# Joining two of the three matmuls of each weight block into one of 512 columns, in the four residual projections of a two-block layer

## The chip, the cores and the metric

The kernel runs on one core of one Trainium2 chip. Its metric is the device time of one execution in microseconds (us), the median of a few runs. Five engines work side by side, each through its own instructions in their written order: TensorE (PE, whose weight loads are listed apart as PEld), VectorE (DVE), ScalarE (ACT), GpSimd (POOL) and SyncE (SP), which here only issues DMA transfers. They wait for each other through semaphores.

## The reference

Two transformer blocks for 256 tokens of width 1024, in float32. What matters here are the four projections whose result is added to the residual stream, and the norm that follows each:

```
# block 1
h = h + merged @ w_out                       # 1024 x 1024   ("wo")
u = rmsnorm(h);  z = silu(u @ w_gate) * (u @ w_up)
h = h + z @ w_ffn_down                       # 2816 x 1024   ("wd")
x = rmsnorm(h)
# block 2
h = rmsnorm(x) * (1 + sc_m) + sh_m
x = x + g_m * (concat(y_ssd, y_att) @ w_out2)   # 1024 x 1024 ("wo2")
h = rmsnorm(x) * (1 + sc_f) + sh_f
x = x + g_f * (conv_ffn(h) )                 # its last product, 2816 x 1024, is "wd2"
return rmsnorm(x)
```

## The kernel before

**Layout and tiling.** Activations are kept with features on the 128 partitions and the 256 tokens (S) along the free dimension, in tiles [128, 8, 256]: eight groups of 128 features. A product is made one output group at a time: `gemm` walks over 128x128 weight blocks and accumulates in one PSUM bank. So wo and wo2 have 8 output groups of 8 blocks, wd and wd2 8 output groups of 22 blocks: 480 blocks in the four projections.

**Split precision.** Each factor is held as a high and a low part in the format fp32r. `wload` fetches 128x1024 weights by DMA (`raw`), ACT rounds them to `wh`, DVE forms the rest `wl` (both tiles have 5 buffers). An activation has a tile for its high part and one for its low part (`xg2h` and `xg2l`, `uf1h` and `uf1l`, and so on). `mm3` makes three matmuls of 256 columns for a block: `wh` by high, `wh` by low, `wl` by high, all into the same 256 columns of the bank. The bank has room for 512.

**Around a residual projection.** When the bank of group f is complete, DVE adds it to the residual (`tt` into `h`, or `stt` into `x1` with the gate as a factor). ACT and DVE then make the high and low part of the scaled group (`scaled`, into `xg2`, `xg3`, `xg4`), and its squares are summed (`Stats`, tile `acc`). The first four products after the norm are made from these scaled but not yet normed groups (96 matmuls, `gemm_multi`, with features 6 and 7 last). In the middle of them PE multiplies `acc` by a matrix of ones, and ACT makes the factor r = exp(-0.5 ln(mean square)) in two instructions. With r, `normed` makes the normed activation group by group: DVE `un`, ACT the high part, DVE the low part (`uf1`, `u2`, `uf2`). The next products read those.

**Order.** The program is recorded, then put in an order by a list scheduler with fixed weights (`OPT`), and each engine gets its instructions in that order. A change of one operation can so move others.

Of the kernel before, what the change touches and what calls it, by code (L numbers as in the profile page):

```python
# [16 lines left out]
P = 128  # L17
S = 256
# [31 lines left out]

# The program is first recorded (operations on symbolic tiles), then put in an order by a list
# scheduler, and then emitted in that order.

# weights of the list scheduler (microseconds; la and altw in nanoseconds)
OPT = dict(
# [13 lines left out]

# products of the first blocks after a norm: the last features come last  # L70
PARTS = [list(range(6)), [6, 7]]
# [70 lines left out]
class Program:  # L142
# [7 lines left out]

    # tiles
    def tile(self, shape, dtype, tag, name, bufs=1, pool="sb"):
# [6 lines left out]

    # operations  # L160
    def op(self, eng, dur, fn, reads, writes, table=None, key=None, nbytes=0):
# [57 lines left out]
    def either(self, out, in_, scale=None, bias=None, func=AF.Copy, key=None):  # L219
        # out = scale * in + bias on ScalarE or on VectorE  # L220
        o = self.act(out, in_, func, bias=bias, scale=scale, key=key)
        nap = sum(isinstance(x, Ref) for x in (bias, scale))
        dur = out.n * (1.0417 if in_.t.psum else 0.5208) + 68 + 61 * nap

        def f():
            v = self.nc.vector
            if scale is None and bias is None:
                v.tensor_copy(out.real(), in_.real())
            elif bias is None:
                v.tensor_scalar(out=out.real(), in0=in_.real(), scalar1=_real(scale), scalar2=None, op0=ALU.mult)  # L230
            elif scale is None:
                v.tensor_scalar(out=out.real(), in0=in_.real(), scalar1=_real(bias), scalar2=None, op0=ALU.add)
            else:
                v.tensor_scalar(out=out.real(), in0=in_.real(), scalar1=_real(scale), scalar2=_real(bias), op0=ALU.mult, op1=ALU.add)

        o.alts["DVE"] = (dur, f, None)
        return o
# [69 lines left out]

    # order
    def schedule(self):
# [31 lines left out]
        def gate(o):  # L341
            # earliest time at which the tiles of o can be had; None when a tag is used up
            g = 0.0
            need = None
            for t in o.tiles:
                if not t.live:
                    k = (t.pool, t.tag)
                    if t.bufs == 1 and t.seq != nxt[k]:
                        return None
                    need = need or defaultdict(int)  # L350
                    need[k] += 1
            if need:
                for k, n in need.items():
                    sf = slot_free[k]
                    if len(sf) < n:
                        return None
                    g = max(g, sorted(sf)[n - 1])
            return g
# [109 lines left out]
def record(pr, d):  # L468
# [13 lines left out]
    def bank2():  # L482
        return bank([P, 2, S])

    def pair(tag, name):
        return big(tag + "h", name + "h", F32R), big(tag + "l", name + "l", F32R)

    def pair_sh(tag, name, m0):
        x = big(tag + "h", name + "h", F32R, [P, KD, S + 2]), big(tag + "l", name + "l", F32R, [P, KD, S + 2])
        sh = mod[:, m0:m0 + 8].rearrange("p (k o) -> p k o", o=1).to_broadcast([P, KD, 2])  # L490
        act(x[0][:, :, S:S + 2], sh, AF.Copy)
        tt(x[1][:, :, S:S + 2], sh, x[0][:, :, S:S + 2].bitcast(F32), ALU.subtract)
        return x

    def hl_of(t):
        return lambda k: (t[0][:, k, :], t[1][:, k, :])

    def memset(t, val):
        pr.op("POOL", 300, lambda: nc.gpsimd.memset(t.real(), val), [], [t], key=-1.0)

    # parameters and constants
    cst_t = pr.tile([P, NCST], F32, "cst", "cst_t")
    vec_t = pr.tile([P, NV], F32, "vec", "vec_t")
    row_t = pr.tile([P, NR0], F32, "row", "row_t")
    bv_t = big("ml", "bv_t", shape=[P, 1152])
    crow = pr.tile([P, D], F32, "crow", "crow")
# [36 lines left out]

    # building blocks
    def wload(src, n):
# [9 lines left out]
    def mm3(ps, w, i, hl, k, first, last):  # L555
        hi, lo = hl(k)
        a, b = w[0][:, i * P:(i + 1) * P], w[1][:, i * P:(i + 1) * P]
        pr.group([(ps, a, hi, first, False), (ps, a, lo, False, False), (ps, b, hi, False, last)])

# [109 lines left out]

    # attention of two heads  # L670
    def attn_pair(q, krows, vcols, bias, init, sink, yh, yl):
# [44 lines left out]

# [1 line left out]
    h = big("h", "h")  # L718
# [19 lines left out]
    def v_third(t3):  # L738
        pv = [bank() for _ in range(2)]
        for c in range(4):  # L740
# [9 lines left out]
            for k2 in range(2):  # L750
                k = 2 * c + k2
                a, b = wh[:, k2 * 384:(k2 + 1) * 384], wl[:, k2 * 384:(k2 + 1) * 384]
                for i in range(2):
                    hi, lo = xg[0][:, k, i * P:(i + 1) * P], xg[1][:, k, i * P:(i + 1) * P]
                    o = pv[i][:, :384]
                    pr.group([(o, hi, a, k == 0, False), (o, hi, b, False, False), (o, lo, a, False, k == 7)])
# [22 lines left out]

    # gates and queries of the recurrence  # L780
    A_all = big("yhh", "A_all", shape=[P, 4, 2, S])
    K_all = big("yhl", "K_all", shape=[P, 4, 2, S])
    Q_all = big("ml", "Q_all", shape=[P, 4, 2, S])
    on = big("mh", "on")
    wi = d["wi"]
# [35 lines left out]
    def hgrn_pair(p):  # L821
# [27 lines left out]
        tt(Q, B, Q, ALU.mult)  # L849
        # scores in blocks of two chunks: within the chunks, then from the second chunk to the first  # L850
        aT = aTs[p % 2]
# [25 lines left out]
        either(ST, ps[:, 0:2])  # L877
        # outputs by token, so that the norm of a head is a scalar of the partition
        o = bank([P, 2, 2, P])
# [58 lines left out]

    # output gate of the recurrence
    hgs = []  # L940
# [8 lines left out]

    # merge of the branches  # L950
    dma(crow, d["rows"][0:1, NR - 1024:NR].to_broadcast([P, D]), D * 512, key=pr.T - 40)
# [33 lines left out]
    for f in range(KD):  # L985
        b = bank2()
        gemm(b[:, 0, :], d["wo"][f], hM)
        tt(h[:, f, :], b[:, 0, :], h[:, f, :], ALU.add)
        scaled(xg, h, gffn, f)
        st2.add(h[:, f, :])  # L990

    def ztiles(name, tags):
        zh = [big(t + "h", f"{name}h{i}", F32R) for i, t in enumerate(tags)]
        zl = [big(t + "l", f"{name}l{i}", F32R) for i, t in enumerate(tags)]
        return zh, zl

# [13 lines left out]
    hl = hl_of(u)  # L1010
    zh, zl = ztiles("z", ("m", "ya", "yh"))
    for p in range(NFF // 2):
# [17 lines left out]
        t, o = divmod(2 * p, 8)  # L1030
        split(zh[t][:, o:o + 2, :], zl[t][:, o:o + 2, :], sg)
    tt(g1e, V("norm_final_g", 0, 8), V("norm_final_g", 0, 8), ALU.mult)
# [6 lines left out]
    st3 = Stats(KD, lambda f: g1e[:, f:f + 1], tail=False)  # L1039
    hz = lambda k, zh=zh, zl=zl: (zh[k // 8][:, k % 8, :], zl[k // 8][:, k % 8, :])  # L1040
    for f in range(KD):
        b = bank2()
        gemm(b[:, 0, :], d["wd"][f], hz, NFF)
        tt(h[:, f, :], b[:, 0, :], h[:, f, :], ALU.add)
        scaled(xg, h, fmix, f)
# [7 lines left out]

# [1 line left out]
    w2 = d["w2"]  # L1055
    xbc = big("yhl", "xbc")
    NG = 4
# [49 lines left out]

    tz = big("yhh", "tz")
    dma(tz, d["toep"], 2048 * 512)
# [5 lines left out]
    for hf in range(2):  # L1115
        pv = [bank() for _ in range(2)]
        for c in range(2):
            wh, wl = wload(d["w2v"][hf, c], 1040)
            for k4 in range(4):
                k = 4 * c + k4  # L1120
                a, b = wh[:, k4 * 260:(k4 + 1) * 260], wl[:, k4 * 260:(k4 + 1) * 260]
                for i in range(2):
                    hi, lo = u[0][:, k, i * P:(i + 1) * P], u[1][:, k, i * P:(i + 1) * P]
                    o = pv[i][:, :260]
# [9 lines left out]
    def ssd():  # L1134
# [48 lines left out]
        either(prev, ps)  # L1183
        m_all = big("mh", "m_all", shape=[P, 2, 2, 4, P])
        ce_all = big("ml", "ce_all", shape=[P, 2, 4, P])
        for i in range(2):
# [69 lines left out]
    ob = [bank2() for _ in range(NG)]  # L1256
    gemm_multi(ws3, [b[:, 0, :] for b in ob], hY, [[4, 5, 6], [7], [0, 1, 2, 3]])
    st4 = Stats(KD, tail=False)
    ffac, sffn = (lambda f: fac[:, 1, f:f + 1]), (lambda f: mod[:, 24 + f:25 + f])
    xg = pair_sh("ya", "xg4", 24)  # L1260
    for f in range(8):
        if f < NG:
            b = ob[f]
        else:
            b = bank2()
            gemm(b[:, 0, :], d["wo2"][f], hY)
        stt(x1[:, f, :], b[:, 0, :], mod[:, 16 + f:17 + f], x1[:, f, :], ALU.mult, ALU.add)
        scaled(xg, x1, ffac, f)
# [7 lines left out]
    with Chain("n4"):  # L1276
        normed(u, x1, ffac, r, sffn)
    zh, zl = ztiles("z2", ("m", "yh", "ya"))
    for f in range(NFF):
# [14 lines left out]
        tt(t[:, 0, :], t[:, 0, :], t[:, 1, :], ALU.mult)  # L1294
        split(zh[f // 8][:, f % 8, :], zl[f // 8][:, f % 8, :], t[:, 0, :])
    st5 = Stats(KD)
    act(rc0, t[:, 0, 0:1], AF.Ln, bias=eps[:, 0:1], scale=0.0)
    hz2 = lambda k: (zh[k // 8][:, k % 8, :], zl[k // 8][:, k % 8, :])
    ot = big("uh", "ot")
    for f in range(8):  # L1300
        b = bank2()
        gemm(b[:, 0, :], d["wd2"][f], hz2, NFF)
        stt(x1[:, f, :], b[:, 0, :], mod[:, 40 + f:41 + f], x1[:, f, :], ALU.mult, ALU.add)
        st5.add(x1[:, f, :])
# [111 lines left out]
```

## Time and profile before

| | |
|---|---|
| median of 3 runs | 804.1 us (803.27 to 804.19) |
| span of the profiled execution | 801.7 us |
| its own time | not given apart; the median stands 2.4 us above the span |
| PE busy | 791.0 us, 99% |
| DVE busy | 604.7 us, 75% |
| ACT busy | 497.3 us, 62% |
| mean granted TensorE clock | 0.997 |

The span runs from the first to the last instruction of the profiled execution. Busy times count overlapped stretches of one engine once. Matmuls overlap each other, so that the duration of one (0.28 us) says little and the distance between two starts says what one costs.

### The profile page before, as it was taken

How to read it: one execution, taken by the hardware profiler on the slowest of the kernel's cores; microseconds unless marked ns; L12 is line 12 of the kernel's file. 1: busy time of each engine (PE TensorE's matmuls, PEld its weight loads, DVE VectorE, ACT ScalarE, POOL GpSimd, SP SyncE). 2: the span in 40 equal slices, each digit the busy share in tenths (PEclk: the TensorE clock that was granted, in tenths of full speed). 3: DMA queues.
4: the chain of work that ended last, by engine and by line, in shares of the span. 5: the costliest groups of instructions: out<-in, count | busy, mean ns of one | idle time of the engine just before them, and what ended most of it. 6: DMA issues, size and time to landing. Idle time of an engine off the chain costs nothing.

```text
span 801.7 us, 16002 instructions
## 1 busy us (share of the span) xinstructions
PE 791.0 (99%) x6362; PEld 759.5 (95%) x6362; DVE 604.7 (75%) x1104; ACT 497.3 (62%) x910; POOL 2.2 (0%) x13
## 2 busy tenths in 40 slices
PE   8999999999999999999999999999999999999996
PEld 7998999899999999999999999977799999999995
DVE  6985876778767788776768869966378988987552
ACT  6688999884445675444444559566466866556451
POOL 1000000000000000000000000000000000000000
PEclk9999999999999999999999999999999999999998
DMA  8945424459787658988778984652334666665731
GB/s 276 334 146 158 126 86 132 131 181 339 259 281 255 183 160 289 328 277 282 261 250 286 327 273 135 190 179 82 97 109 138 202 200 209 200 181 148 214 94 53
DMA packets 47803, 161.39 MB, mean 201 GB/s; under 512 B 5600, under 2 KB 8304, under 8 KB 47600
## 3 DMA queue, kind: packets, MB, share of 16 engines
q1 hardware_dynamic: 47728, 160.37, 62.6%
q8 instruction: 50, 0.82, 0.4%
q14 instruction: 25, 0.20, 0.1%
HBM read 159.03 MB, written 1.06 MB: 200 GB/s over the span
## 4 chain that ended last, share of the span: by engine, by line
PE 97%; DMA 1%; SPq 1%; DVE 0%; ACT 0%; issue 0%; DVEq 0%
PE ps L292 87%; PE ps L284 8%; PE ps L299 2%; DMA raw<-in_wv_dram 1%; SPq L305 1%; DVE ot L255 0%; DVE wl L255 0%; ACT r L215 0%; ACT wh L215 0%; DVE x L261 0%; ACT sql L215 0%; DVEq L1411 0%
## 5 line engine op out<-in xcount | busy, mean ns | idle before, releaser
L215 ACT ACTIVATE wh<-raw 128x1024 fp32r<-128x1024 f32 (+3 forms) x253 | 256.9, 1021 | 211.1 <-PE ps L292 144.1
L255 DVE TENSOR_TENSOR wl<-raw,wh 128x1024 fp32r<-128x1024 f32 (+3 forms) x257 | 300.3, 1175 | 81.8 <-ACT wh L215 78.1
L292 PE MATMUL ps<-u1h,wh 128*128 128x256 f32 x360 | 106.8, 297 | 0.0
L292 PE MATMUL ps<-u1h,wl 128*128 128x256 f32 x360 | 101.3, 281 | 0.0
L292 PE MATMUL ps<-u1l,wh 128*128 128x256 f32 x360 | 101.0, 280 | 0.0
L292 PE MATMUL ps<-uf2h,wl 128*128 128x256 f32 x320 | 90.1, 282 | 0.0
L292 PE MATMUL ps<-uf1h,wl 128*128 128x256 f32 x320 | 90.1, 282 | 0.0
L292 PE MATMUL ps<-uf2h,wh 128*128 128x256 f32 x320 | 89.8, 281 | 0.0
L292 PE MATMUL ps<-uf1h,wh 128*128 128x256 f32 x320 | 89.8, 280 | 0.0
L292 PE MATMUL ps<-uf1l,wh 128*128 128x256 f32 x320 | 89.7, 280 | 0.0
L292 PE MATMUL ps<-uf2l,wh 128*128 128x256 f32 x320 | 89.7, 280 | 0.0
L261 DVE SCALAR_TENSOR_TENSOR raw<-raw,crow 128x1024 f32<-128x1024 f32 x48 | 58.5, 1222 | 40.5 <-DMA raw<-in_wada_dram 40.4
L292 PEld LDWEIGHTS ps<-u1h,wh 128*128 128x128 f32 x360 | 68.0, 189 | 2.2 <-issue 1.5
L292 PEld LDWEIGHTS ps<-u1l,wh 128*128 128x128 f32 x360 | 67.9, 189 | 0.0
L292 PEld LDWEIGHTS ps<-u1h,wl 128*128 128x128 f32 x360 | 67.7, 188 | 0.0
L292 PEld LDWEIGHTS ps<-uf1h,wh 128*128 128x128 f32 x320 | 60.6, 189 | 0.0
L292 PEld LDWEIGHTS ps<-uf2h,wh 128*128 128x128 f32 x320 | 60.5, 189 | 0.0
L292 PEld LDWEIGHTS ps<-uf2l,wh 128*128 128x128 f32 x320 | 60.2, 188 | 0.0
L292 PEld LDWEIGHTS ps<-uf1l,wh 128*128 128x128 f32 x320 | 60.2, 188 | 0.0
L292 PEld LDWEIGHTS ps<-uf2h,wl 128*128 128x128 f32 x320 | 60.1, 188 | 0.0
L292 PEld LDWEIGHTS ps<-uf1h,wl 128*128 128x128 f32 x320 | 60.1, 188 | 0.0
L292 PE MATMUL ps<-zh,wh 128*128 128x256 f32 x176 | 49.5, 281 | 0.0
(320 smaller groups left out, 2048.0 us busy)
## 6 DMA issues: line engine op xcount, KB each, us to landing
raw<-in_wi_dram SPq DMA_DIRECT2D x49, 512.0 KB, 4.6
raw<-in_wada_dram SPq DMA_DIRECT2D x48, 512.0 KB, 4.6
raw<-in_wup_dram SPq DMA_DIRECT2D x44, 512.0 KB, 4.3
raw<-in_wd_dram SPq DMA_DIRECT2D x32, 512.0 KB, 4.3
raw<-in_wg_dram SPq DMA_DIRECT2D x22, 512.0 KB, 4.5
raw<-in_wu_dram SPq DMA_DIRECT2D x22, 512.0 KB, 5.0
raw<-in_w_dram SPq DMA_DIRECT2D x20, 512.0 KB, 4.4
raw<-in_wo_dram SPq DMA_DIRECT2D x16, 512.0 KB, 3.7
```

The source lines that it names most:

```text
L215: self.nc.scalar.activation(out.real(), in_.real(), func, **kw)
L255: f = lambda: self.nc.vector.tensor_tensor(out=out.real(), in0=in0.real(), in1=in1.real(), op=op)
L261: self.nc.vector.scalar_tensor_tensor(out=out.real(), in0=in0.real(), scalar=_real(scalar), in1=in1.real(), op0=op0, op1=op1, **kw)
L284: f = lambda: self.nc.tensor.matmul(out.real(), lhsT.real(), rhs.real(), start=start, stop=stop)
L292: self.nc.tensor.matmul(out.real(), a.real(), b.real(), start=start, stop=stop)
L299: f = lambda: self.nc.tensor.transpose(out.real(), in_.real(), ident.real())
L305: f = lambda: self.nc.sync.dma_start(out=_real(out), in_=_real(src))
```

## The change

High and low part of an activation become the two halves of one tile [128, 8, 2, 256]. Where the PSUM tile given to `mm3` has 512 columns, one matmul multiplies `wh` by both parts, the high part's products going to the bank's first half and the low part's to its second, and the matmul of `wl` by the high part goes to the second half. The bank is then added to the residual in two instructions, one for each half. This is done in wo, wd, wo2 and wd2; all other products keep three matmuls of 256 columns. Tiles that shared buffers with the two parts (`A_all` and `K_all`, `xbc` and `tz`, and others) are joined in pairs in the same way. `OPT` is the same.

```diff
-        hi, lo = hl(k)
+        hi, lo, both = hl(k)
         a, b = w[0][:, i * P:(i + 1) * P], w[1][:, i * P:(i + 1) * P]
-        pr.group([(ps, a, hi, first, False), (ps, a, lo, False, False), (ps, b, hi, False, last)])
+        if ps.n == 2 * S:
+            calls = [(ps, a, both, first, last), (ps[:, 1, :], b, hi, False, False)]
+            pr.group(calls[::-1] if last else calls)
+        else:
+            pr.group([(ps, a, hi, first, False), (ps, a, lo, False, False), (ps, b, hi, False, last)])
...
-        gemm(b[:, 0, :], d["wo"][f], hM)
-        tt(h[:, f, :], b[:, 0, :], h[:, f, :], ALU.add)
+        gemm(b, d["wo"][f], hM)
+        for e in range(2):
+            tt(h[:, f, :], b[:, e, :], h[:, f, :], ALU.add)
...
-        gemm(b[:, 0, :], d["wd2"][f], hz2, NFF)
-        stt(x1[:, f, :], b[:, 0, :], mod[:, 40 + f:41 + f], x1[:, f, :], ALU.mult, ALU.add)
+        gemm(b, d["wd2"][f], hz2, NFF)
+        for e in range(2):
+            stt(x1[:, f, :], b[:, e, :], mod[:, 40 + f:41 + f], x1[:, f, :], ALU.mult, ALU.add)
```

The order of the instructions moves at the two places where wo and wo2 hand over to the feed-forward products.

DVE behind wo, before: from the last sum of squares on, r is used in `un`, and `uf1l` is the low part of the normed activation.

```order
L261 SCALAR_TENSOR_TENSOR un<-h,vec_t,r 128x256 x3
L255 TENSOR_TENSOR uf1l<-un,uf1h 128x256 x3
L261 SCALAR_TENSOR_TENSOR un<-h,vec_t,r 128x256 x3
L255 TENSOR_TENSOR uf1l<-un,uf1h 128x256 x2
L261 SCALAR_TENSOR_TENSOR un<-h,vec_t,r 128x256 x2
L255 TENSOR_TENSOR uf1l<-un,uf1h 128x256 x3
L255 TENSOR_TENSOR wl<-raw,wh 128x1024 x3
```

The same place now (`uf_3686` is the joined tile of both parts):

```order
L261 SCALAR_TENSOR_TENSOR un<-h,vec_t,r 128x256 x3
L255 TENSOR_TENSOR sg<-ps,r 128x256
L255 TENSOR_TENSOR wl<-raw,wh 128x1024
L255 TENSOR_TENSOR uf_3686<-un,uf_3686 128x256 x3
L261 SCALAR_TENSOR_TENSOR un<-h,vec_t,r 128x256 x3
L255 TENSOR_TENSOR wl<-raw,wh 128x1024
L255 TENSOR_TENSOR uf_3686<-un,uf_3686 128x256 x3
L261 SCALAR_TENSOR_TENSOR un<-h,vec_t,r 128x256 x2
L255 TENSOR_TENSOR wl<-raw,wh 128x1024
L255 TENSOR_TENSOR uf_3686<-un,uf_3686 128x256 x2
```

Three weight roundings and one product with r, which stood behind the whole normed activation, now stand between its parts.

ACT behind wo2, before: the two steps of r, then the high parts of the normed activation (`uf2h`).

```order
L215 ACTIVATE r<-ps,eps 128x256
L215 ACTIVATE r<-r 128x256
L215 ACTIVATE uf2h<-un,mod 128x256 x6
L215 ACTIVATE wh<-raw 128x1024 x2
L215 ACTIVATE uf2h<-un,mod 128x256 x2
```

And now:

```order
L215 ACTIVATE wh<-raw 128x1024
L215 ACTIVATE r<-ps,eps 128x256
L215 ACTIVATE wh<-raw 128x1024
L215 ACTIVATE r<-r 128x256
L215 ACTIVATE wh<-raw 128x1024 x2
L215 ACTIVATE uf_7286<-un,mod 128x256 x8
```

Four weight roundings, two of them behind the first high parts before, now stand ahead of all of them. On DVE in the same place two roundings stand ahead of the first `un`, one behind it.

PE behind wo2, now: from the product of the squares with ones (`acc_7001`) to the first matmuls of the normed activation.

```order
L284 MATMUL ps<-acc_7001,ones_d 128x256
L292 MATMUL ps<-xg_6876,wh 128x258 x2
L292 MATMUL ps<-xg_6876,wl 128x258
L292 MATMUL ps<-xg_6876,wh 128x258 x2
L292 MATMUL ps<-xg_6876,wl 128x258
L292 MATMUL ps<-xg_6876,wh 128x258 x2
L292 MATMUL ps<-xg_6876,wl 128x258
L292 MATMUL ps<-xg_6876,wh 128x258 x2
L292 MATMUL ps<-xg_6876,wl 128x258
L292 MATMUL ps<-uf_7286,wh 128x256 x2
```

Of the 96 matmuls with the unnormed `xg`, 84 now stand ahead of the product with ones and 12 behind it; before, 39 stood ahead and 57 behind. Behind wo it is 66 and 30 now, and was 36 and 60. Behind wd it is 36 and 60 in both. In both kernels the block order behind the 12 (or 30) is: three blocks of the first normed product, some of the second, and only then the first product's groups 3 to 7, with 14 blocks in all up to group 7.

## Rows read from the trace of the kernel before

**Rows 1.** The page: span, and the first engines' busy time, share and instructions.

```profile
span 801.7 us, 16002 instructions
...
PE 791.0 (99%) x6362; PEld 759.5 (95%) x6362; DVE 604.7 (75%) x1104; ACT 497.3 (62%) x910; POOL 2.2 (0%) x13
```

**Rows 2.** The chain that ended last, in order of time: start, us, what.

```profile
290.45 0.43 PE ps L284 x2
290.88 187.64 PE ps L292 x1584
...
793.17 0.49 DVE x L261
...
794.16 0.71 PE ps L284 x2
```

**Rows 3.** Timeline of PE, 20 to 22 us, first and last of 13 rows: start, us.

```profile
19.82 0.34 PE L292 MATMUL ps<-wh,xg1l 128*128 128x384 f32 x1
...
21.91 0.33 PE L292 MATMUL ps<-wh,xg1l 128*128 128x384 f32 x1
```

**Rows 4.** The waits, longest first: us in total, times, longest.

```profile
ACT wh L215 <- PE ps L292: 144.1, 114, 2.9
```

**Rows 5.** Busy time by stretch, wo: us, then PE, PEld, DVE, ACT, POOL, clock, DMA.

```profile
263.30:286.00 22.70, 22.70 (x194) 22.70 (x193) 17.91 (x31) 14.10 (x24) 0.00 (x0) 1.00 0.63 185
```

**Rows 6.** Timeline of DVE behind wo: start, us, instruction.

```profile
287.27 0.42 DVE L255 TENSOR_TENSOR h<-ps,h 128x256 f32<-128x256 f32 x1
287.60 1.21 DVE L255 TENSOR_TENSOR wl<-raw,wh 128x1024 fp32r<-128x1024 f32 x1
...
292.32 1.27 DVE L261 SCALAR_TENSOR_TENSOR un<-h,vec_t,r 128x256 f32<-128x256 f32 x3
293.51 1.09 DVE L255 TENSOR_TENSOR uf1l<-un,uf1h 128x256 fp32r<-128x256 f32 x3
294.52 1.27 DVE L261 SCALAR_TENSOR_TENSOR un<-h,vec_t,r 128x256 f32<-128x256 f32 x3
...
298.18 3.49 DVE L255 TENSOR_TENSOR wl<-raw,wh 128x1024 fp32r<-128x1024 f32 x3
```

**Rows 7.** Timeline of PE behind wo: first unnormed, product with ones, first normed.

```profile
286.05 0.28 PE L292 MATMUL ps<-xg2h,wh 128*128 128x256 f32 x1
...
290.28 0.59 PE L284 MATMUL ps<-acc,ones_d 128*128 128x256 f32 x2
...
297.82 0.28 PE L292 MATMUL ps<-uf1h,wh 128*128 128x256 f32 x1
```

**Rows 8.** Timeline of ACT behind wo and behind wo2.

```profile
290.92 0.47 ACT L215 ACTIVATE r<-ps,eps 128x256 f32<-128x256 f32 x1 [1.08 <-PE ps L284]
...
610.11 0.47 ACT L215 ACTIVATE r<-ps,eps 128x256 f32<-128x256 f32 x1 [2.04 <-PE ps L284]
...
615.18 1.99 ACT L215 ACTIVATE wh<-raw 128x1024 fp32r<-128x1024 f32 x2
```

**Rows 9.** Timeline of DVE behind wo2.

```profile
611.07 1.28 DVE L261 SCALAR_TENSOR_TENSOR un<-x,fac,r 128x256 f32<-128x256 f32 x3 [1.26 <-ACT r L215]
612.26 1.27 DVE L261 SCALAR_TENSOR_TENSOR uf2l<-un,mod,uf2h 128x256 fp32r<-128x256 f32 x3
```

**Rows 10.** Timeline of PE behind wo2, the three places of Rows 7.

```profile
604.81 0.28 PE L292 MATMUL ps<-xg4h,wh 128*128 128x258 f32 x1
...
609.48 0.60 PE L284 MATMUL ps<-acc,ones_d 128*128 128x256 f32 x2
...
616.74 0.29 PE L292 MATMUL ps<-uf2h,wh 128*128 128x256 f32 x1
```

**Rows 11.** Timeline of DVE behind wd.

```profile
474.26 0.42 DVE L255 TENSOR_TENSOR h<-ps,h 128x256 f32<-128x256 f32 x1
475.26 1.23 DVE L255 TENSOR_TENSOR wl<-raw,wh 128x1024 fp32r<-128x1024 f32 x1 [0.58 <-ACT wh L215]
```

**Rows 12.** Busy time by stretch, end of the span, columns as in Rows 5.

```profile
797.00:798.00 1.00, 0.00 (x0) 0.00 (x0) 1.00 (x3) 0.00 (x0) 0.00 (x0) 0.77 0.75 248
```

More of the change, by code (lines that the diff above doesn't have):

```diff
@@ L483, in bank2, with halves @@
         return bank([P, 2, S])
+    def halves(x):
+        return x[:, :, 0, :], x[:, :, 1, :], x
     def pair(tag, name):
-        return big(tag + "h", name + "h", F32R), big(tag + "l", name + "l", F32R)
+        return halves(big(tag, name, F32R, [P, KD, 2, S]))
     def pair_sh(tag, name, m0):
-        x = big(tag + "h", name + "h", F32R, [P, KD, S + 2]), big(tag + "l", name + "l", F32R, [P, KD, S + 2])
+        x = halves(big(tag, name, F32R, [P, KD, 2, S + 2]))
         sh = mod[:, m0:m0 + 8].rearrange("p (k o) -> p k o", o=1).to_broadcast([P, KD, 2])
@@ L495, in hl_of @@
     def hl_of(t):
-        return lambda k: (t[0][:, k, :], t[1][:, k, :])
+        return lambda k: tuple(x[:, k] for x in t)
     def memset(t, val):
@@ L504, in record @@
     row_t = pr.tile([P, NR0], F32, "row", "row_t")
-    bv_t = big("ml", "bv_t", shape=[P, 1152])
+    bv_t = big("m", "bv_t", shape=[P, 1152])
     crow = pr.tile([P, D], F32, "crow", "crow")
@@ L753, in v_third @@
                 for i in range(2):
-                    hi, lo = xg[0][:, k, i * P:(i + 1) * P], xg[1][:, k, i * P:(i + 1) * P]
+                    hi, lo = (x[:, k, i * P:(i + 1) * P] for x in xg[:2])
                     o = pv[i][:, :384]
@@ L778, in record @@
     hl = hl_of(u)
[L781 to L784, printed above, removed]
+    AK = big("yh", "AK", shape=[P, 2, 4, 2, S])
+    A_all, K_all = AK[:, 0], AK[:, 1]
+    QO = big("m", "QO", shape=[P, 2, KD, S])
+    Q_all, on = QO[:, 0].rearrange("p (a b) s -> p a b s", b=2), QO[:, 1]
     wi = d["wi"]
@@ L992, in ztiles @@
     def ztiles(name, tags):
-        zh = [big(t + "h", f"{name}h{i}", F32R) for i, t in enumerate(tags)]
-        zl = [big(t + "l", f"{name}l{i}", F32R) for i, t in enumerate(tags)]
-        return zh, zl
+        return [pair(t, f"{name}{i}") for i, t in enumerate(tags)]
     hx = hl_of(xg)
@@ L1010, in record @@
     hl = hl_of(u)
-    zh, zl = ztiles("z", ("m", "ya", "yh"))
+    z = ztiles("z", ("m", "ya", "yh"))
     for p in range(NFF // 2):
@@ L1030, in record @@
         t, o = divmod(2 * p, 8)
-        split(zh[t][:, o:o + 2, :], zl[t][:, o:o + 2, :], sg)
+        split(z[t][0][:, o:o + 2, :], z[t][1][:, o:o + 2, :], sg)
     tt(g1e, V("norm_final_g", 0, 8), V("norm_final_g", 0, 8), ALU.mult)
@@ L1039, in record @@
     st3 = Stats(KD, lambda f: g1e[:, f:f + 1], tail=False)
-    hz = lambda k, zh=zh, zl=zl: (zh[k // 8][:, k % 8, :], zl[k // 8][:, k % 8, :])
+    hz = lambda k, z=z: hl_of(z[k // 8])(k % 8)
     for f in range(KD):
         b = bank2()
-        gemm(b[:, 0, :], d["wd"][f], hz, NFF)
-        tt(h[:, f, :], b[:, 0, :], h[:, f, :], ALU.add)
+        gemm(b, d["wd"][f], hz, NFF)
+        for e in range(2):
+            tt(h[:, f, :], b[:, e, :], h[:, f, :], ALU.add)
         scaled(xg, h, fmix, f)
@@ L1055, in record @@
     w2 = d["w2"]
-    xbc = big("yhl", "xbc")
+    xt = big("yh", "xt", shape=[P, 2, KD, S])
+    xbc, tz = xt[:, 0], xt[:, 1]
     NG = 4
@@ L1106, in gates @@
             act(sz[:, 2 * p:2 * p + 2, :], b, AF.Silu)
-    tz = big("yhh", "tz")
     dma(tz, d["toep"], 2048 * 512)
@@ L1122, in record @@
                 for i in range(2):
-                    hi, lo = u[0][:, k, i * P:(i + 1) * P], u[1][:, k, i * P:(i + 1) * P]
+                    hi, lo = (x[:, k, i * P:(i + 1) * P] for x in u[:2])
                     o = pv[i][:, :260]
@@ L1183, in ssd @@
         either(prev, ps)
-        m_all = big("mh", "m_all", shape=[P, 2, 2, 4, P])
-        ce_all = big("ml", "ce_all", shape=[P, 2, 4, P])
+        mc = big("m", "mc", shape=[P, 6, 4, P])
+        m_all = mc[:, 0:4].rearrange("p (i g) e t -> p i g e t", i=2)
+        ce_all = mc[:, 4:6]
         for i in range(2):
@@ L1256, in record @@
     ob = [bank2() for _ in range(NG)]
-    gemm_multi(ws3, [b[:, 0, :] for b in ob], hY, [[4, 5, 6], [7], [0, 1, 2, 3]])
+    gemm_multi(ws3, ob, hY, [[4, 5, 6], [7], [0, 1, 2, 3]])
     st4 = Stats(KD, tail=False)
@@ L1265, in record @@
             b = bank2()
-            gemm(b[:, 0, :], d["wo2"][f], hY)
-        stt(x1[:, f, :], b[:, 0, :], mod[:, 16 + f:17 + f], x1[:, f, :], ALU.mult, ALU.add)
+            gemm(b, d["wo2"][f], hY)
+        for e in range(2):
+            stt(x1[:, f, :], b[:, e, :], mod[:, 16 + f:17 + f], x1[:, f, :], ALU.mult, ALU.add)
         scaled(xg, x1, ffac, f)
@@ L1277, in record @@
         normed(u, x1, ffac, r, sffn)
-    zh, zl = ztiles("z2", ("m", "yh", "ya"))
+    z = ztiles("z2", ("m", "yh", "ya"))
     for f in range(NFF):
@@ L1294, in record @@
         tt(t[:, 0, :], t[:, 0, :], t[:, 1, :], ALU.mult)
-        split(zh[f // 8][:, f % 8, :], zl[f // 8][:, f % 8, :], t[:, 0, :])
+        split(z[f // 8][0][:, f % 8, :], z[f // 8][1][:, f % 8, :], t[:, 0, :])
     st5 = Stats(KD)
     act(rc0, t[:, 0, 0:1], AF.Ln, bias=eps[:, 0:1], scale=0.0)
-    hz2 = lambda k: (zh[k // 8][:, k % 8, :], zl[k // 8][:, k % 8, :])
-    ot = big("uh", "ot")
+    hz2 = lambda k: hl_of(z[k // 8])(k % 8)
+    ot = big("u", "ot")
     for f in range(8):
         b = bank2()
-        gemm(b[:, 0, :], d["wd2"][f], hz2, NFF)
-        stt(x1[:, f, :], b[:, 0, :], mod[:, 40 + f:41 + f], x1[:, f, :], ALU.mult, ALU.add)
+        gemm(b, d["wd2"][f], hz2, NFF)
+        for e in range(2):
+            stt(x1[:, f, :], b[:, e, :], mod[:, 40 + f:41 + f], x1[:, f, :], ALU.mult, ALU.add)
         st5.add(x1[:, f, :])
```

## The prediction

> **What bounds the kernel now.** I read the page first: PE is busy for 791.0 of 801.7 us [rows 1]. As matmuls overlap, this alone does not say that PE sets the pace, so I read the chain of waits next: two pieces of it run for hundreds of us as matmul behind matmul without a gap, the one between wo and the next norm being 1584 matmuls in 187.64 us [rows 2]. That is 118.5 ns for a matmul of 256 columns. The other engines run ahead of PE: most of ACT's idle time before a weight rounding is a wait for PE to give a buffer back, 144.1 us in all [rows 4]. So every ns taken from a matmul is gained, and every wait put in front of PE is lost in full. Only the ends of the four projections are different: there PE needs the norm, which DVE and ACT make. In this trace the 36 unnormed matmuls ahead of the product with ones and the 60 behind it cover that: PE reaches the first normed matmul 7.5 us after that product [rows 7], 7.3 us behind wo2 [rows 10], and does not wait.
>
> **What the merge gives.** There are 480 blocks. Each loses two matmuls of 256 columns (236.9 ns) and gets one of 512. No row has 512 columns. The nearest is 384: 13 starts from 19.82 to 21.91, so 174.2 ns each [rows 3]. From 256 to 384 columns a matmul grows by 55.7 ns; drawn on, 512 columns cost 229.9 ns, and a block gains 7.0 ns. The other reading is a fixed part on top of one column per cycle: the granted clock is 1.00, which is the level of 2.4 GHz [rows 5], so 256 columns need 106.7 ns and 11.8 ns are fixed; 512 then cost 225.1 and a block gains 11.8 ns. The sum takes the middle, 9.4 ns: 480 x 9.4 = 4.5 us (3.4 to 5.7). Farther bounds: nothing, if time goes by columns alone; and 215 ns for 512 columns, which is half of the 0.43 us that two float32 records of 256 columns take [rows 2], worth 21.9 ns or 10.5 us. I do not take the second, since 384 columns already lie 14 ns above one column per cycle.
>
> The Trainium skill (TensorE: Matmul & The Clock Gate, "Back-to-back issue gap") gives N/2.4 + 2.5 ns for a warm matmul, so a merged pair would save only 2.5 ns, 1.2 us for 480. The trace differs: 118.5 ns stand where the rule has 109.2. By the rule's saving the forecast would be some 3 us higher, still inside the range.
>
> **What the second addition costs.** 16 additions into `h` and 16 into `x1` are new on DVE. The first kind steps by 0.33 us (287.27 to 287.60 [rows 6]), the second by 0.40 (1.19 for three of that form [rows 9]): 16 x 0.33 + 16 x 0.40 = 11.7 us. Inside the projections this is covered. DVE is busy 17.91 of 22.70 us in wo, where the additions stand densest [rows 5], and 8 x 0.33 = 2.6 us fit; if the cover were gone, PE would wait for a `wl`, at up to 1.16 us a time (three in 3.49 [rows 6]). At the very end nothing covers it: the last `stt` at 793.17 heads the chain of squares, ones, r and output [rows 2], so 0.4 us are lost. Behind wd the order is unchanged, and DVE idles 0.58 us before the `wl` that follows the last addition [rows 11], where the second addition fits: nothing.
>
> **What the moved order costs.** This is the larger term, and the diff does not show it. Behind wo and wo2 the product with ones now has fewer matmuls behind it, and weight roundings stand between r and the normed groups.
>
> *Behind wo.* Count from ACT's first step of r, which starts 0.64 us after the product with ones starts (290.28 to 290.92 [rows 7, 8]). The product takes PE 0.43 us, the 30 matmuls left 3.55, so PE is at the first normed block at 3.34 and, with 14 blocks of three matmuls (355 ns) up to group 7, would be done at 8.3. DVE can start `un` 0.96 after ACT's first step (610.11 to 611.07 [rows 8, 9]). Its list is now: three `un` 1.19 and three low parts 1.01 (292.32, 293.51, 294.52 [rows 6]), both twice, then two `un` 0.79 and two low parts 0.75; between them three `wl` of 1.16 and one product with r at 0.33. Sum 2 x 2.20 + 0.79 + 0.75 + 3.48 + 0.33 = 9.75, so the last low part is there at 10.7; with its two last matmuls PE is done at 11.0. PE loses 2.7 us.
>
> *Behind wo2.* Count from the start of the product with ones. PE resumes at 0.43, makes 12 matmuls of 119.5 ns, is at the first normed block at 1.86 and would finish 14 blocks at 6.8. ACT gets the first free weight buffer at about 0.2 and rounds (1.0 us, half of 1.99 [rows 8]); the first step of r runs from 1.2 to 1.7, a rounding to 2.7, the second step to 3.1, two roundings to 5.1, and the first high part is there at 5.5. DVE's second `wl` waits for the rounding at 2.7 and ends at 3.9. From there: `un` 1.19, `wl` 1.16, low 1.19, `un` 1.19, low 1.19, two `un` 0.79, one product with r 0.33, two low parts 0.87 (steps of [rows 9]): 7.9, so 11.8, and PE is done at 12.0. PE loses 5.2 us. Ahead of this, the scaled groups come late (ACT rounds three weights before group 4), but groups 0 to 3 of three products stand first on PE and cover it.
>
> **Sum.** -4.5 + 2.7 + 5.2 + 0.4 = +3.8 us. On the span of 801.7 [rows 1] that is 805.5; the median of the runs is 804.1, 2.4 us above the span, and with the same difference the forecast is **807.9 us**. About 0.2% (1.6 us) is what a measurement of this kernel can tell from no change, so this is slower.
>
> **Rivals.**
> - *The waits do not come* (0.12): the semaphores let PE run on because ACT and DVE are further ahead than I count. For it: before, PE never waits here. Against it: the new order is strict on each engine, and 12 matmuls cannot cover 7 us. It decides in the other direction when the two losses stay under 2.5 us together. Time 804.1 - 4.5 + 0.4 = 800.0, faster.
> - *Only one of the two waits comes* (0.13): 805.3 with that behind wo2, 802.7 with that behind wo.
> - *The merge gives all* (0.08): 512 columns at 215 ns, with both waits: 804.1 - 10.5 + 8.3 = 801.9. Against it stand the 384-column rows.
> - *The merge gives nothing* (0.07): 512 columns at 236.9 ns, so the change does not do what it says: 804.1 + 8.3 = 812.4. For it: the cost grows nearly with columns (118.5 to 174.2 is 1.47 for 1.5). Against it: it is not quite 1.5.
> - *The clock falls behind wo2* (0.15, with the forecast's other terms): PE would idle 3.6 us there, from 1.9 to 5.5. At the end of this trace the last matmul ends at 794.87 [rows 2], and the clock's mean over 797 to 798 is 0.77 [rows 12]: it fell there from 1.00 to 0.50, the level of 1.2 GHz, with no matmul since 794.87. Matmuls then cost twice as much until it rises. No row shows how long that takes; 14 blocks at half speed need 10 us instead of 5, of which 3.3 would show beyond the wait for DVE, so 0 to 3.3; I take 1.5: 809.4, up to 811.2. The Trainium skill (the same page, "HAM oscillation") says that gaps between bursts of matmuls bring the half rate back; the end of this trace agrees.
> - The forecast itself, 806.7 to 809.0 by the two readings of the matmul: 0.45.
>
> **Range and chances.** 802.0 to 812.0 leaves out the case without waits and about half of the case without gain, some 0.16. Slower by over 0.2%: forecast 0.45, clock 0.15, no gain 0.07, a little of the single wait 0.03: 0.70. Faster by over 0.2% (below 802.5): no waits 0.12, most of the full gain 0.06: 0.18. Within 0.2%: 0.12.
>
> **What would show it.** A 512-column matmul followed by its start-to-start distance: 225 to 230 ns is right, 237 or 215 wrong. Inside wd and wd2 PE should run without gaps, 176 blocks in 176 x 0.3554 - 176 x 0.0094 = 60.9 us each. Behind wo a hole of 2 to 4 us spread over the first 14 normed blocks, with PE waiting for DVE; behind wo2 one of 4 to 7 us, whose first part, 3.6 us, is empty and ends with ACT's first high part. The chain of waits should leave PE there for DVE's `wl` and `uf` and ACT's `wh`. At the end 0.4 us more between the last matmul and the output. The forecast is wrong if `un` starts sooner after r than its place in the order allows, if PE finds matmuls of later products to fill the holes, or if further holes open inside the projections.

## The result and the profile after

The changed kernel takes 810.6 us (median of 4 runs, 810.28 to 811.03), the kernel before 803.7 beside it: ratio 1.0088, 95% interval 1.0074 to 1.0101. It is slower, by 6.9 us instead of the 3.8 of the forecast. The first lines of the page after, as [rows 1]:

```profile
span 808.8 us, 15078 instructions
...
PE 791.6 (98%) x5882; PEld 737.1 (91%) x5882; DVE 617.6 (76%) x1138; ACT 498.0 (62%) x908; POOL 2.2 (0%) x13
```

PE has 480 instructions fewer and is busy as long as before: the busy time alone doesn't show where the time went. To see it, I took the first matmul of each product from the two traces and compared the stretches between them (us):

| from first matmul to first matmul | before | after | difference |
|---|---|---|---|
| start to wo | 263.27 | 262.15 | -1.12 |
| wo | 22.78 | 22.42 | -0.36 |
| unnormed products behind wo | 11.77 | 11.86 | +0.09 |
| normed products of block 1 | 113.63 | 116.25 | +2.62 |
| wd | 62.59 | 62.85 | +0.26 |
| from wd's end on, with the first 16 of wo2's 64 blocks | 110.09 | 109.99 | -0.10 |
| wo2, the other 48 blocks | 20.68 | 20.56 | -0.12 |
| unnormed products behind wo2 | 11.93 | 15.21 | +3.28 |
| normed products of block 2 | 113.63 | 116.78 | +3.15 |
| wd2, to its last matmul | 62.48 | 61.12 | -1.36 |
| last matmul to the end | 8.84 | 9.57 | +0.73 |

The sum is 7.1, the difference of the spans. The stretch up to wo holds no changed matmul; in the ten profiles with joined tiles wo starts between 262.15 and 262.97, so the scatter alone is 0.8 us there, and I read nothing into it. (The one profile of before, 263.27, lies beyond all ten; whether the joined tiles have a part in that stays open.)

**The merged matmul.** Timeline of PE inside wd (start, us, instruction):

```profile
439.77 0.28 PE L292 MATMUL ps<-z,wl 128*128 128x256 f32 x1
439.89 0.39 PE L292 MATMUL ps<-z,wh 128*128 128x512 f32 x1
...
441.86 0.28 PE L292 MATMUL ps<-z,wl 128*128 128x256 f32 x1
```

Six blocks lie between 439.77 and 441.86. Over the whole of the four projections, pauses left out, the next matmul starts 232.1 ns behind the start of one of 512 columns and 117.5 ns behind one of 256: 349.6 a block, where it was 355.4. The gain is 5.8 ns a block, 2.8 us for 480.

**Behind wo.** The chain of waits there (start, us, what):

```profile
292.53 0.54 PE ps L284 x2
...
293.59 0.43 ACT r L215
...
295.66 1.13 DVE wl L255
296.79 1.01 DVE uf L255 x3
...
298.11 0.87 DVE un L261 x2
298.99 1.15 DVE wl L255
...
300.18 0.39 PE ps L292
```

In the kernel before the chain at this place is nothing but matmuls [rows 2]. Now it leaves PE for r, DVE's `un`, and two `wl` that stand between the groups. PE has two pauses there (the idle time in brackets, with what ended it), and the longer one ends with the second `wl` itself:

```profile
297.18 0.38 PE L292 MATMUL ps<-uf,wh 128*128 128x256 f32 x1 [0.48 <-DVE uf L255]
...
300.18 0.39 PE L292 MATMUL ps<-uf,wl 128*128 128x256 f32 x1 [1.54 <-DVE wl L255]
```

**Behind wo2.** Timeline of PE, the last unnormed matmul and the first two normed ones:

```profile
617.93 0.28 PE L292 MATMUL ps<-xg,wl 128*128 128x258 f32 x1
621.29 0.58 PE L292 MATMUL ps<-uf,wh 128*128 128x256 f32 x1 [3.08 <-ACT uf L215]
622.67 0.58 PE L292 MATMUL ps<-uf,wh 128*128 128x256 f32 x1 [0.80 <-DVE uf L261]
```

PE waits for ACT's first high part and then for DVE's first low part. These matmuls take 0.58 us instead of 0.28. Busy time by stretch, columns as in [rows 5], says why: the seventh number is the granted clock.

```profile
619.00:620.00 1.00, 0.00 (x0) 0.00 (x0) 1.00 (x2) 1.00 (x2) 0.00 (x0) 1.00 0.21 20
620.00:621.00 1.00, 0.00 (x0) 0.00 (x0) 1.00 (x3) 1.00 (x2) 0.00 (x0) 0.58 0.67 266
621.00:622.00 1.00, 0.58 (x1) 0.29 (x1) 1.00 (x2) 1.00 (x3) 0.00 (x0) 0.50 0.87 291
...
626.00:627.00 1.00, 1.00 (x7) 1.00 (x6) 1.00 (x4) 0.79 (x2) 0.00 (x0) 0.51 0.00 0
627.00:628.00 1.00, 1.00 (x11) 1.00 (x11) 1.00 (x4) 0.97 (x3) 0.00 (x0) 1.00 0.00 0
```

It fell to 0.50, the level of 1.2 GHz, while PE had no matmul, and came back at 627, after matmuls had run without a pause since 622.67. The Trainium skill (TensorE: Matmul & The Clock Gate, "HAM oscillation") says that gaps between bursts of matmuls bring the half rate back; these rows agree.

**In front of wd** there is a hole that the forecast did not have. The timelines of DVE and then of PE:

```profile
417.14 1.23 DVE L261 SCALAR_TENSOR_TENSOR raw<-raw,crow 128x1024 f32<-128x1024 f32 x1 [3.26 <-DMA raw<-in_wada_dram]
418.29 0.08 DVE L261 DVE_READ_ACCUMULATOR raw<-raw,crow 128x1 f32 x1
418.29 0.69 DVE L255 TENSOR_TENSOR sg<-ps,sg 128x512 f32<-128x512 f32 x1
```

```profile
420.85 0.50 PE L292 MATMUL ps<-z,wh 128*128 128x512 f32 x1 [1.03 <-DVE z L255]
```

DVE waits 3.26 us for a row of the conditioning weights; behind it in DVE's order stands the `sg` from which the last feature of `z` is made. Before, the same wait is 3.15 us long but ends before PE needs `z`.

**The end.** The chain of waits (the row of before is 793.17 in [rows 2], one `x` of 0.49 instead of two):

```profile
799.62 0.49 DVE x L261
...
800.14 0.50 DVE x L261
```

### The profile page after: what moved, and what is told of

The parts are those of the page before. It is cut to its first block, busy times and chain, and to the rows that moved or that the text cites. A ratio compares the mean times of both kernels' runs of the same rounds, so it can differ in the third digit from the quotient of the medians.

```text
span 808.8 us, 15078 instructions
## 1 busy us (share of the span) xinstructions
PE 791.6 (98%) x5882; PEld 737.1 (91%) x5882; DVE 617.6 (76%) x1138; ACT 498.0 (62%) x908; POOL 2.2 (0%) x13
## 4 chain that ended last, share of the span: by engine, by line
PE 92%; DVE 3%; DMA 3%; ACT 1%; issue 1%; SPq 1%; DVEq 0%
PE ps L292 83%; PE ps L284 8%; PE ps L299 2%; DMA raw<-in_wada_dram 1%; DVE wl L255 1%; DMA raw<-in_wv_dram 1%; DVE un L261 1%; SPq L305 1%; ACT r L215 0%; DVE raw L261 0%; DVE ot L255 0%; ACT wh L215 0%; ACT L464 0%; DVE uf L255 0%; DVE x L261 0%
## 5 line engine op out<-in xcount | busy, mean ns | idle before, releaser
L292 PE MATMUL ps<-uf,wh 128*128 128x256 f32 x1280 | 230.0, 282 | 4.4 <-ACT uf L215 3.1
L292 PEld LDWEIGHTS ps<-uf,wh 128*128 128x128 f32 x1280 | 198.0, 190 | 5.1 <-ACT uf L215 3.3
L292 PE MATMUL ps<-u,wh 128*128 128x256 f32 x976 | 188.1, 291 | 0.0
L292 PE MATMUL ps<-uf,wl 128*128 128x256 f32 x640 | 180.4, 282 | 1.5 <-DVE wl L255 1.5
L292 PEld LDWEIGHTS ps<-u,wh 128*128 128x128 f32 x976 | 149.5, 189 | 9.1 <-issue 8.1
L292 PE MATMUL ps<-u,wl 128*128 128x256 f32 x488 | 136.9, 281 | 0.0
L292 PE MATMUL ps<-z,wh 128*128 128x512 f32 x352 | 122.2, 394 | 1.0 <-DVE z L255 1.0
L292 PEld LDWEIGHTS ps<-uf,wl 128*128 128x128 f32 x640 | 121.2, 189 | 1.7 <-DVE wl L255 1.7
L292 PE MATMUL ps<-z,wl 128*128 128x256 f32 x352 | 95.8, 279 | 0.0
L292 PEld LDWEIGHTS ps<-u,wl 128*128 128x128 f32 x488 | 91.8, 188 | 0.0
```

Source lines behind the costliest of these rows:

```text
L292: self.nc.tensor.matmul(out.real(), a.real(), b.real(), start=start, stop=stop)
```

## The experiments

Times are medians; ratios are to runs of the kernel before on the same chip, with 95% intervals. Where an order is called the same, every engine has its instructions in the same sequence.

**1. The order of before, with the whole change.** What moved the order are the 16 additions in wo and wo2 as operations of their own: given to the scheduler as one operation of the old length, they leave each engine with the order of before.

```diff
-        for e in range(2):
-            tt(h[:, f, :], b[:, e, :], h[:, f, :], ALU.add)
+        pr.both(h[:, f, :], b, h[:, f, :])   # one operation that issues both additions
...                                            # the same in wd, wo2 and wd2
```

> The merged matmuls and both additions stay; the two additions of a group are given to the scheduler as one operation of the old length, so that every engine has the order of the kernel before. Theory (the loss is the moved order): the gain of the merge, 480 x 5.7 ns = 2.8 us, comes out, less some 0.7 us at the end: 801.6 us, 800.8 to 802.4, and no hole of PE behind wo and wo2 longer than 0.5 us. Rival (the loss is the second addition itself, which makes the sum of squares late wherever the product with ones stands): PE then waits at that product, up to 8 x 0.33 us behind wo and 8 x 0.40 us behind wo2 less the 0.8 us that it had in hand before: 801.6 + 1.8 + 2.4 = 805.8, 804 to 807. Rival (joined tiles or 512 columns slow something else): 808 or more, whatever the order.

Measured: 806.3 us (804.24 to 807.6), 1.0034 (1.0021 to 1.0046). My theory of that moment, that the moved order is the whole loss, fell, and the rival came: PE waits, 0.92 us at the product with ones behind wo and 1.29 for a scaled group behind wo2. Timelines of PE at the two places:

```profile
290.65 0.67 PE L297 MATMUL ps<-acc,ones_d 128*128 128x256 f32 x2 [0.92 <-DVE acc L255]
...
611.05 0.39 PE L305 MATMUL ps<-xg,wh 128*128 128x258 f32 x1 [1.29 <-DVE xg L261]
```

From the first unnormed matmul to the first behind the product with ones it is now 5.65 us behind wo and 7.16 behind wo2, where it was 4.48 and 4.91: 3.4 us more. The late transfer in front of wd fell into this profile too (1.66 us from start to start). Timeline of DVE at the end of wo:

```profile
287.76 0.87 DVE L283 TENSOR_TENSOR h<-ps,h 128x256 f32<-128x256 f32 x2
288.56 1.22 DVE L255 TENSOR_TENSOR wl<-raw,wh 128x1024 fp32r<-128x1024 f32 x1
...
290.08 0.42 DVE L255 TENSOR_TENSOR acc<-acc,sq 128x256 f32<-128x256 f32 x1
```

The two additions take 0.80 us up to the next instruction, one took 0.33 (287.27 to 287.60 [rows 6]). Side by side, a second addition therefore costs 0.47, not 0.33: it reads what the first writes, and starts 0.45 behind it, when that has ended. The changed kernel doesn't pay this: its order puts other instructions between the two additions of a group, and two additions of different groups step by 0.33 there. The same place in its trace:

```profile
286.90 0.75 DVE L255 TENSOR_TENSOR h<-ps,h 128x256 f32<-128x256 f32 x2
287.57 1.21 DVE L255 TENSOR_TENSOR wl<-raw,wh 128x1024 fp32r<-128x1024 f32 x1
```

So run 1 doesn't only restore the order, it also makes the additions dearer by 0.14 us a group; how much of its loss that is, no run separates.

**2. Three matmuls in the order of the changed kernel.**

```diff
-            calls = [(ps, a, both, first, last), (ps[:, 1, :], b, hi, False, False)]
-            pr.group(calls[::-1] if last else calls)
+            pr.group([(ps[:, 0, :], a, hi, first, False), (ps[:, 1, :], a, lo, False, False), (ps[:, 1, :], b, hi, False, last)])
```

> The order of the changed kernel with its joined tiles and two additions, but three matmuls of 256 columns for a block in place of 512 and 256. Theory (the merge gives 5.7 ns for a block): 810.6 + 2.8 = 813.4 us, 812.4 to 814.2, the holes behind wo and wo2 as in the changed kernel. Rival (the shorter block only moved the waiting elsewhere, since the holes are set by DVE and ACT): 810.6 to 811.5.

Measured: 814.1 us (812.93 to 814.99), 1.0132 (1.0117 to 1.0147). Against the changed kernel the merge is worth 0.44%, some 3.5 us; 2.8 lies within the two intervals. The gain of the merge is real and does reach the end time, but the pair is no clean measure of its size, since the two profiles differ elsewhere too. The changed kernel's has the hole in front of wd; run 2's has none there, but one at the product with ones behind wo. In this order a row of conditioning weights stands on DVE ahead of the last scaled group. Its transfer came late, and PE waited for the sum. Timelines of DVE and of PE:

```profile
292.67 1.22 DVE L261 SCALAR_TENSOR_TENSOR raw<-raw,crow 128x1024 f32<-128x1024 f32 x1 [2.21 <-DMA raw<-in_wada_dram]
...
294.69 0.70 PE L284 MATMUL ps<-acc,ones_d 128*128 128x256 f32 x2 [1.12 <-DVE acc L255]
```

**3. Three matmuls in the order of before**, the edits of 1 and 2 together.

> The order of the kernel before, joined tiles and two additions, three matmuls of 256 columns for a block: everything of the change but the merge and the moved order. Theory: the additions and the joined tiles cost only the end: 803.7 + 0.7 = 804.4 us, 803.7 to 805.0. Rival (the second additions hold up PE): 803.7 + 0.7 + 1.8 + 2.4 = 808.6, 806 to 809. The difference to the run with merge and the same order is the merge by itself: 2.8 us expected, 4.5 by the prediction's reading.

Measured: 806.9 us (805.56 to 810.74), 1.0046 (1.0028 to 1.0063). The rival is nearer: the second additions, side by side, cost 3 us without any merge, by the same two waits (0.93 and 1.29 us of idle PE). The difference to run 1 is only 0.6, within the scatter: over half of the merge's gain is swallowed in run 1's profile by the late transfer, so this pair doesn't measure the merge. By stretches it does: wd takes 62.40 us here and 61.53 in run 5 below.

**4. Unused matmuls in the hole behind wo2.**

```diff
+FILL = 24
...
+                pre = [(ps, fill[:, 0, 0:P], fill[:, 0, :S], True, True)] * FILL if fill is not None and k0 + i == 0 else ()
...
-            gemm(b[:, 0, :], wup[f], hl)
+            gemm(b[:, 0, :], wup[f], hl, fill=xg[0] if 2 * f == NG else None)
```

> The changed kernel with 24 unused matmuls of 256 columns (24 x 118.4 ns = 2.84 us) on PE ahead of the first normed matmul behind wo2, where PE idles 3.1 us; their products are overwritten. Theory (the half clock behind wo2 costs time of its own): the granted clock stays at 1.00 there and 1.2 to 2.0 us come back: 809.0 us, 808.6 to 809.4. Rival (what follows the hole waits for DVE and ACT anyway, so that the half clock is hidden): clock at 1.00, time 810.6 plus or minus 0.4. If the clock falls all the same, the fill is too short or starts too late.

Measured: 809.3 us (808.37 to 810.88), 1.0073 (1.0061 to 1.0085), 1.3 less than the changed kernel. Busy time by stretch, now with the clock at 1.00 throughout:

```profile
620.00:621.00 1.00, 0.66 (x4) 0.26 (x2) 1.00 (x2) 1.00 (x4) 0.00 (x0) 1.00 0.93 365
621.00:622.00 1.00, 0.14 (x1) 0.14 (x2) 1.00 (x3) 0.23 (x1) 0.00 (x0) 1.00 0.98 303
...
626.00:627.00 1.00, 1.00 (x10) 0.97 (x9) 1.00 (x4) 0.97 (x3) 0.00 (x0) 1.00 0.00 0
```

The normed products of block 2 take 115.34 us instead of 116.78, so the half clock cost 1.4; the wait for the first normed matmul is as long as it was (15.22 from the first unnormed one). The stretch shows this, not the medians: their intervals overlap, and the hole in front of wd, 1.3 us in the changed kernel's profile, is absent from this one.

**5. to 7. Where the loss sits.** Run 5 merges wd and wd2 alone, in the order of before; run 6 is run 5 with the last group of wd2 left at three matmuls and one addition; run 7 merges wo and wo2 alone, with the additions as separate operations.

```diff
-        gemm(b, d["wo"][f], hM)            # runs 5 and 6, the same for wo2; run 7 for wd and wd2
+        gemm(b[:, 0, :], d["wo"][f], hM)   # and one addition
...
+        if f < 7:                          # run 6: wd2 merged for seven groups of eight
...
```

> The merge in wd and wd2 alone (352 of the 480 blocks); wo and wo2 have three matmuls a block and one addition as before, tiles are joined, and the order of every engine is that of the kernel before. Theory (the loss sits in wo and wo2, where the second additions make the sum of squares and the scaled groups late; in wd and wd2 a group has 22 blocks to cover them): 803.3 - 352 x 5.7 ns + 0.7 at the end = 802.0 us, 801.3 to 802.6, in executions without the late transfer in front of wd, which adds 1.3 to 1.7. No hole of PE behind wo and wo2. Rival (joined tiles and additions cost time wherever they are): 804 or more.

> As the run with the merge in wd and wd2 alone, but the last of the eight groups of wd2 keeps three matmuls a block and one addition. Theory (the end loses what a second addition takes there): 0.5 to 0.7 us come back and 22 x 5.7 ns are lost: 801.4 us, 800.8 to 802.0, from the last matmul of wd2 to the end as before. Rival (the later end has another cause than the second addition): as the other run, 802.0.

> The merge in wo and wo2 alone (128 blocks), with two additions each given to the scheduler as two operations, so that the products with ones stand where the changed kernel has them; wd and wd2 as before. Theory (the whole loss belongs to wo and wo2): 803.3 - 0.7 + 2.7 + 6.4 = 811.7 us, 810.8 to 812.6, slower than the full change by the 2 us of gain in wd and wd2 less the end. Rival (part of the loss comes from wd and wd2): 808 to 810.

Measured: run 5 801.5 us (0.9962, 0.9947 to 0.9977), run 6 800.8 (0.9956, 0.9937 to 0.9975), run 7 812.1 (1.0095, 1.0067 to 1.0122). Runs 5 and 7 came out as the theory had them, run 6 just at the lower edge of its range. In run 7's profile the clock fell behind wo as well: it was 0.50 from 301, and the normed products of block 1 took 117.49 us, where they took 116.25 in the changed kernel, whose clock stayed at 1.00 there. Run 5 takes 61.53 us for wd, 176 blocks of 349.6 ns. Its chain of waits at the end has two additions, that of run 6 one; first run 5:

```profile
790.58 0.49 DVE x L285
...
791.10 0.49 DVE x L285
...
791.61 0.42 ACT sql L215
```

and run 6:

```profile
791.96 0.49 DVE x L261
...
792.48 0.42 ACT sql L215
```

From the first addition to `sql` it is 1.03 us against 0.52. Run 6 gives this back, but its median differs from run 5 by no more than the intervals allow. Runs 5 and 6 both beat the kernel before.

**8. and 9. Order and additions apart.** Both merge all four projections and leave out the second addition in wo and wo2: the products of the low activations and of the low weights are then missing from the residual there. Run 8 has the order of before; run 9 that of the changed kernel, the additions being left out after the order is set.

```diff
+        pr.both(h[:, f, :], b, h[:, f, :], n=1)    # run 8: the first half only
...
+        tt(h[:, f, :], b[:, 0, :], h[:, f, :], ALU.add)
+        skip(h[:, f, :], b[:, 1, :])               # run 9: planned, not issued
```

> All four projections merged, order of the kernel before, but in wo and wo2 the second half of the bank isn't added: the products of the low activations and of the low weights are left out of the residual there, and DVE has one addition per group. Theory (the waits of PE behind wo and wo2 in that order, 1.2 and 2.2 us, come from the second additions on DVE): they vanish, the sum of squares is there before the product with ones, 803.4 - 2.8 + 0.7 = 801.3 us, up to 802.8 where the late transfer in front of wd falls into the execution. Rival (the waits come from the 512-column matmuls, which let PE reach the product earlier, or from the joined tiles): 804.5 to 806.5.

> The changed kernel with its own order, the same second additions of wo and wo2 left out of the program after the order is set (so the same products are missing from the residual). Theory (once the order is set, what PE loses counts from the product with ones, which stands at 66 and 84 matmuls whether the sum of squares is there or not): the holes behind wo and wo2 stay, 810.6 us, 809.5 to 811. Rival (the additions themselves make the holes, and the order is only where they show): 804 to 807.

Measured: run 8 801.2 us (0.9962, 0.9947 to 0.9977), run 9 810.5 (1.0072, 1.0047 to 1.0098). With the two kernels above this makes a square:

| ratio to before | second additions of wo and wo2 issued | left out |
|---|---|---|
| order of before | 1.0034 (run 1) | 0.9962 (run 8) |
| order of the change | 1.0088 (the change) | 1.0072 (run 9) |

In run 8 the sum of squares is there earlier, and PE takes the product with ones without a wait. Timelines of DVE and of PE:

```profile
286.78 0.42 DVE L283 TENSOR_TENSOR h<-ps,h 128x256 f32<-128x256 f32 x1
287.12 1.22 DVE L255 TENSOR_TENSOR wl<-raw,wh 128x1024 fp32r<-128x1024 f32 x1
...
288.64 0.42 DVE L255 TENSOR_TENSOR acc<-acc,sq 128x256 f32<-128x256 f32 x1
```

```profile
289.56 0.59 PE L297 MATMUL ps<-acc,ones_d 128*128 128x256 f32 x2
```

The last sum starts at 288.64 against 290.08 in run 1, and PE came to the product at 289.6 in both. Run 9 issues as few additions, and yet PE's holes are those of the changed kernel, 3.08 us behind wo2:

```profile
621.35 0.38 PE L292 MATMUL ps<-uf,wh 128*128 128x256 f32 x1 [3.08 <-ACT uf L215]
622.73 0.39 PE L292 MATMUL ps<-uf,wh 128*128 128x256 f32 x1 [1.00 <-DVE uf L261]
```

The clock falls there in run 9 too, from 1.00 to 0.50 between 623 and 624. So there are two prices, and they don't add. In the old order PE pays for what the additions make late, the sum of squares behind wo and the last scaled groups behind wo2: 3.4 us. (Runs 1 and 8 lie 0.0072 apart, some 5.8 us; 1.7 more are the late transfer in run 1's profile, and the rest is not accounted for.) The new order puts the product with ones so late that the sum is there in the changed kernel, though behind wo with only 0.15 us in hand (its last sum ends at 292.23, the product starts at 292.38), and not in run 2, where a transfer was late. It pays for the short cover behind the product: 9.1 us by the stretches of the table (2.7 behind wo, 6.4 behind wo2), additions or not. Timelines of the changed kernel behind wo, DVE's last sum and PE's product with ones:

```profile
291.81 0.42 DVE L255 TENSOR_TENSOR acc<-acc,sq 128x256 f32<-128x256 f32 x1
...
292.38 0.67 PE L284 MATMUL ps<-acc,ones_d 128*128 128x256 f32 x2
```

## Why the prediction came out as it did

**What bounds the kernel: right.** The ns taken off the matmuls of wd and wd2 reached the end time: run 5 is 2.0 us faster, with an interval of 1.2 us to either side, where 352 x 5.8 ns less 0.5 at the end make 1.5. And the stretches behind wo and wo2 are longer by what PE waited there.

**What the merge gives: mis-sized.** "The sum takes the middle, 9.4 ns: 480 x 9.4 = 4.5 us (3.4 to 5.7)". It was 5.8 ns and 2.8 us, outside the two readings: 512 columns cost 232 ns, above both 229.9 and 225.1. Drawing the line on from 256 and 384 was the better reading, and even it was 2 ns short. The Trainium skill's spacing (TensorE: Matmul & The Clock Gate, "Back-to-back issue gap"), which that section states for a matmul by itself, gives 215.8 ns for 512 columns, an estimate by its formula that the trace doesn't bear out; the 2.5 ns that it saves per joined pair was too low by about as much as my 9.4 was too high.

**What the second addition costs: right in the sum, with luck.** "Inside the projections this is covered ... 8 x 0.33 = 2.6 us fit". For the changed kernel the covered term holds: an addition steps by 0.33 there, and leaving the additions out moves the ratio by 0.0016, inside the intervals (run 9). But I looked for the price in the wrong place. What a second addition delays is not `wl` but the sum of squares and the scaled groups; with the additions side by side the last sum comes 1.44 us later at the end of wo, and in the order of before that costs 3.4 us (runs 1 and 8). I looked at DVE's mean load in wo, 17.91 of 22.70 us [rows 5], where I should have followed one chain, addition, scaled group, square, sum, to the product with ones. Before, the last sum had 0.7 us in hand to the product at 290.28 [rows 7]. Timeline of DVE before:

```profile
289.13 0.42 DVE L255 TENSOR_TENSOR acc<-acc,sq 128x256 f32<-128x256 f32 x1
```

In the changed kernel the moved order covers it, with 0.15 us in hand.

**Behind wo: right in the sum, the last wait another.** 2.7 us forecast, 0.09 + 2.62 measured, with the two `wl` in the chain of waits and PE waiting for DVE, as listed. DVE's list came out too: the last low part is there 10.6 us after r's first step, 10.7 in the forecast. But PE, which was to wait for that part, did not wait for it. Its longer pause, 1.54 us, came earlier and was for a `wl`, whose matmul stands between the first normed groups; behind it PE reached the last part about when it was ready. Timeline of DVE, the last two low parts:

```profile
302.97 0.76 DVE L255 TENSOR_TENSOR uf<-un,uf 128x256 fp32r<-128x256 f32 x2
```

**Behind wo2: the wait right, the clock a rival that came.** 5.2 forecast, 6.4 measured, of which 1.4 is the half clock (run 4): 5.0 remain. The rival with the clock took 1.5 for it. It deserved more than 0.15, since the empty stretch that brings the clock down was part of the forecast itself, 3.6 us there and 3.1 idle in the trace. (The rival with the wait behind wo2 alone adds up to 805.2, not 805.3.)

**The end: mis-sized.** 0.4 forecast, 0.5 in the chain, 0.7 from the last matmul. The second `stt` waits for the first and takes its whole 0.50, where I counted a step of 0.40 in a row of independent ones.

**Not seen: the transfer in front of wd**, +1.3 us in this profile. In run 1's profile, where the hole is 1.66, the chain of waits shows two transfers of the conditioning weights one after the other, the second issued when DVE has worked off the first and the `wl` behind it:

```profile
399.56 5.93 DMA raw<-in_wada_dram
...
410.87 5.62 DMA raw<-in_wada_dram
```

Before, DVE had the two rows at 404.04 and 414.44 after issues at 399.26 and 409.31, 4.8 and 5.1 us, against 6.0 and 5.7 by the same measure in run 1 and 7.1 and 5.2 in the changed kernel. The hole stands in three of the seven profiles with a merged wd and in none of the four without. Whether the merge has a part in it, or only the length of two transfers, stays open.

**Sum.** 3.8 forecast, 7.1 in the spans: 1.7 from the merge, 1.2 behind wo2, 1.3 in front of wd and 0.3 at the end are 4.5 more, less 1.1 in the stretch up to wo, which the change doesn't explain.

## What to carry to other kernels

A step that saves time on the pacing engine and adds a little on another is first weighed on the chain that feeds the next stage: in the order of before, one more DVE addition for each group made the sum of squares and the scaled groups late, and the projections with few matmuls a group (8 blocks, 2.8 us) couldn't cover it, while those with 22 blocks could. So make such a change where the cover is long and leave it out where it is short: run 6 keeps 330 of the 480 merges and is 0.4% faster than before. And where a scheduler sets the order, hold the order fixed first and change it second; otherwise two effects are timed as one. Look then at what the means of holding it change by themselves, as the additions side by side did here.

## What was not expected of the hardware

At a granted clock of 1.00 an fp32r matmul of 512 columns stands 232 ns from the next, one of 384 columns 174 and one of 256 columns 118: the cost per column hardly falls with size. Two dependent DVE additions of 256 columns cost 0.80 us where a single one steps by 0.33. The clock behind wo2 fell 2.2 us after the start of the last unnormed matmul in the changed kernel (617.93; down at 620.2, as the 0.58 of that stretch has it) and only after 623 in run 9 (last one at 617.99), with the order of PE's matmuls and the pauses behind the unnormed ones alike; and behind wo it fell in run 7 and stayed at 1.00 in the changed kernel, at the same pause of 1.54 us. So the pauses there don't alone say when it falls. And with 24 useless matmuls in an empty stretch of PE the clock stayed at 1.00 for the useful ones behind them, and that stretch was 1.4 us shorter.
